# A 64-token tile's high and low parts side by side as one 128-column stationary, in a streaming encoder layer

## The chip, the cores and the metric

The kernel runs on one core of a Trainium2 chip. The metric is the device time of one execution in microseconds. Three runs of the kernel before took 2988.57, 2991.18 and 2994.07 us; their median, 2991.18 us, is the time that the prediction starts from. One further execution was recorded by the hardware profiler; its span, from the first to the last instruction, is 2988.4 us.

## What is computed

One layer of a streaming encoder, in float32, for 2048 prompt tokens and 64 sample tokens, with a model width of 1024:

```python
h = rms_norm(x, norm1_g) * (1 + sc1) + sh1
z = h @ w_in                                  # GLU pair, q, k, v, two gates
conv_out, conv_state = conv_module(u, conv_hist, ...)
attn_out = attend(q, k, v).reshape(B, T, ATTN_DIM) @ w_attn_out
merged = sigmoid(g_conv) * conv_out + sigmoid(g_attn) * attn_out
x = x + gt1 * (merged @ w_o)                  # output projection
h2 = rms_norm(x, norm2_g) * (1 + sc2) + sh2
gate, up = split(h2 @ w_ffn_in)
x = x + gt2 * ((silu(gate) * up) @ w_ffn_out) # second FFN product
```

Prompt and sample have vectors of their own for the modulation (`sc1` to `gt2`) and share all weights. The two lines with a comment on the right behind `x =` are those that the change touches, and of their rows only the 64 sample tokens.

## The kernel before

**Products in three passes.** Matmuls run in the format fp32r, whose operands hold fewer bits than float32. So each operand is kept as two tensors: `hi`, the value rounded by an ACT copy, and `lo`, what is left, which DVE (or POOL, for weights) makes by a subtraction (`split`, lines 706 to 709; `Weights.split`, lines 451 to 505, for weights). A product is then three matmuls into the same PSUM bank, hi by hi, hi by lo and lo by hi (`mm3`, lines 700 to 704); lo by lo is left out. Each of the three loads its stationary operand anew.

**Two parts.** The first part (to line 1657) computes the input projection, the convolution and the attention in four token blocks and stores gates and mixer outputs in HBM. The second part (from line 1660) goes over three blocks, `CBLOCKS`: tokens 0 to 576, 576 to 1344 and 1344 to 2112. Tokens 0 to 63 are the sample; they are a tile of their own, of 64 tokens, in the first block. All other tiles have 128. The first block has five tiles, the others six each.

**A block of the second part** (the loop at line 1802) has these steps:

- *Merge and output projection*, in two chunks of tiles. For each of eight groups of 128 channels, `merge` (lines 1677 to 1699) multiplies the mixer outputs `cin` by their weights, applies the gates, and splits the result into `m[0]` (hi) and `m[1]` (lo), 128 channels by the tokens of the chunk. `wo` (lines 1836 to 1846) takes a tile's columns of `m` as the stationary operand and 512 columns of `w_o` as the moving one; the PSUM banks are called `pw`. In the first chunk of the first block the tiles are 64, 128 and 128 tokens.
- *Residual* (lines 1710 to 1796), one generator for each tile: DVE multiplies the two banks by `gt1`, adds `x`; ACT squares and sums; DVE and POOL make the reciprocal root; ACT scales; PE transposes the tile to channels by tokens; ACT and DVE modulate and split it. For the sample tile the transposes are `pt<-ident,xn` of 64x64.
- *First FFN product* (`up`, lines 1926 to 1980), row by row: 22 rows of 128 hidden channels, `f`. Each row is made by a Strassen-like scheme for two by two blocks, with the tokens split into two halves of 288 (first block) or 384; the sample tokens are in half 0. The results are called `y` and `z` and lie in PSUM banks (`ps`). `hidden` (lines 1900 to 1903) splits a row's half into the tile `hid`, hi and lo, 128 channels by tokens.
- *Second FFN product*. In the first block (`add_down`, lines 2136 to 2168) two rows at a time: for each tile and each of two 512-column halves of `w_ffn_out`, 2 x 3 matmuls with `hid` as the stationary operand into a bank called `pd`, which ACT copies (first pair) or DVE adds (all later ones) into `acc` in SBUF. The last four rows are done together at the end of the block; there DVE adds `acc`, multiplies by `gt2`, adds `x1`, and the tile is written out. The other two blocks do most rows by `down_pair`, which the change does not touch.

**What sets the order.** PE's program order is written by the code as it runs. `Meter` estimates each operation's time as it is recorded, `Stream` keeps a clock for each engine, and the lanes' generators (weight loads, residual steps and others) are advanced when their due time has come on PE's clock. Whether the low part of a weight is made by POOL or by DVE is decided by the same clocks (line 483). A scheduler below then places instructions by readiness. So a change of a few matmuls also moves other instructions nearby. Loads and stores go by the queue of SP, in its own order.

Weights wait in HBM; they are loaded raw into staging buffers, split into `whi` and `wlo`, of which five pairs exist, and a pair comes free when PE has done its last matmul with it.

The functions that the diff touches:

Of the kernel before, what the change touches and what calls it, by code (L numbers as in the profile page):

```python
# [8 lines left out]
F32 = mybir.dt.float32  # L9
# [9 lines left out]
KT = 8  # L19
# [592 lines left out]
def streaming_layer(ctx: ExitStack, tc: tile.TileContext, I, O):  # L612
# [87 lines left out]
    def mm3(ps, lh, ll, rh, rl, first, last, **kw):  # L700
        pe.matmul(ps, lh, rh, start=first, stop=False, **kw)
        pe.matmul(ps, lh, rl, start=False, stop=False, **kw)
        pe.matmul(ps, ll, rh, start=False, stop=last, **kw)
        stream.spend()

    def split(hi, lo, src):
        act.activation(hi, src, AF.Copy)
        stream.after("dve", "act")
        dve.tensor_tensor(lo, src, hi.bitcast(F32), ALU.subtract)
# [966 lines left out]

    def merge(c0, c1, src, m, ahead, load):
        n = c1 - c0
        for ct in range(KT):
            g = ahead.pop(0)  # L1680
            if ct == 2 and load:
                load()
            wh, wl = W.get(("ca", ct))
            ps = [
                columns(
                    kts(wh, 4 * j, 4 * j + 4), kts(wl, 4 * j, 4 * j + 4), kts(src[0][j], 0, 4), kts(src[1][j], 0, 4), 0, n
                )[:, :n]
                for j in range(2)
            ]
            t = piece("t1", "t1")[:, :n]  # L1690
            stream.after("dve", "pe")
            dve.scalar_tensor_tensor(t, g[0][:, :n], 1.0, ps[0], ALU.add, ALU.mult)
            dve.scalar_tensor_tensor(ps[1], g[1][:, :n], 1.0, ps[1], ALU.add, ALU.mult)
            W.done()
            if ct + 2 < KT:
                ahead.append(gate_columns(c0, c1, ct + 2))
            dve.scalar_tensor_tensor(ps[1], ps[1], 2.0, t, ALU.mult, ALU.add)
            stream.after("act", "dve")
            split(m[0][:, ct, :n], m[1][:, ct, :n], ps[1])


    Y = ("y0", "z0", "y1", "z1")
# [7 lines left out]
    def residual(pp, t, n, gt1, a, half, hs, free, last, i):  # L1710


        which = int(t < SMP)
        x_t = [wk.tile([P, 512], F32, tag="ws", name="x_t", bufs=4) for _ in range(2)]
        for j in range(2):
            nc.sync.dma_start(x_t[j][:n], rows(x_p, x_s, t, n)[:, 512 * j : 512 * j + 512])
        yield
        x1 = token_row("x1")
        for j in range(2):
            f = slice(512 * j, 512 * j + 512)  # L1720
            stream.after("dve", "pe")
            dve.tensor_tensor(pp[j][:n], pp[j][:n], gt1[which][:n, f], ALU.mult)
        hs["rows"] -= 1
        yield
        for j in range(2):
            f = slice(512 * j, 512 * j + 512)
            dve.tensor_tensor(x1[:n, f], pp[j][:n], x_t[j][:n], ALU.add)
        free()
        yield stream.when("dve")
        xn = token_row("xn")  # L1730
        ssq = wk.tile([P, 1], F32, tag="ssq", bufs=2)
        act.activation(xn[:n], x1[:n], AF.Square, accum_out=ssq[:n])
        nc.sync.dma_start(x1_d[t : t + n], x1[:n])
        yield stream.when("act")
        r = rsqrt_mean(wk, ssq[:n], n, 1, D, 4)

        W.behind = lambda ins=gps.last.ins: tc.issue_after(ins)
        yield stream.when("pool")
        stream.after("act", "pool")
        act.activation(xn[:n], x1[:n], AF.Copy, scale=r)  # L1740
        yield stream.when("act")

        pts = pp if last else [bank_of(Y[i % 2 * 2 + j], "pt") for j in range(2)]
        pts = [pt.rearrange("p (k n) -> p k n", k=4) for pt in pts]
        for kk in range(KT):
# [12 lines left out]
        hs["columns"] -= 1  # L1758
        yield stream.when("dve", "act")
        for c, e, o in ((0, min(n, half - a), a), (max(0, half - a), n, max(0, a - half))):  # L1760
            if c >= e:
                continue
            b = [x[:, :, c:e] for x in cols_]
            at = lambda name: [hs[name][j][:, :, o : o + e - c] for j in range(2)]
            as_f32 = lambda name: [x.bitcast(F32) for x in at(name)]
            if a + c < half:
                for g in range(2):
                    split(*at("b%d1" % (g + 1)), b[g])
                    yield stream.when("dve")
# [12 lines left out]
            act.activation(at("b22")[0], b[1], AF.Copy)  # L1782
            for x in as_f32("b11"):
                dve.tensor_tensor(b[0], b[0], x, ALU.subtract)
            dve.tensor_tensor(at("t3")[1], t, as_f32("t3")[0], ALU.subtract)
            dve.tensor_tensor(t, b[1], b[0], ALU.subtract)
            yield stream.when("dve")
            split(*at("t2"), t)
            split(*at("t1"), b[0])
            yield stream.when("dve")  # L1790
            dve.tensor_tensor(b[0], as_f32("b21")[0], t, ALU.subtract)
            dve.tensor_tensor(b[0], b[0], as_f32("b21")[1], ALU.add)
            dve.tensor_tensor(at("b22")[1], b[1], as_f32("b22")[0], ALU.subtract)
            yield stream.when("dve")
            split(*at("t4"), b[0])
            yield stream.when("act")
# [5 lines left out]
    for s, (lo, hi) in enumerate(CBLOCKS):  # L1802
# [4 lines left out]
        for i, (c0, c1) in enumerate(chunks):  # L1807
# [28 lines left out]
            def wo(i, k):  # L1836
                (t, n), pp = grp[i], pss[i]
                if k not in ws:
                    ws[k] = W.get(("wo", k))
                wh, wl = ws[k]  # L1840
                c = slice(t - c0, t - c0 + n)
                for j in range(2):
                    f = slice(512 * j, 512 * j + 512)
                    mm3(pp[j][:n], m[0][:, k, c], m[1][:, k, c], wh[:, 0, f], wl[:, 0, f], k == 0, k == KT - 1)
                if i == len(grp) - 1:
                    W.done()

# [50 lines left out]
            return hid[i][:, f % 2]  # L1898

        def hidden(f, i, ps):  # L1900
            hi, lo = (hid_of(f)[:, j, i * half : (i + 1) * half] for j in range(2))
            stream.after("act", "dve")
            split(hi, lo, ps)

        class Operands:

# [229 lines left out]
        def add_down(fs, ws):  # L2136

            last = fs[-1] == NF - 1
            for i, (t, n) in enumerate(tiles):
# [6 lines left out]
                for e, j in [(e, j) for e in fs for j in range(2)] if last and not i else [(e, j) for j in range(2) for e in fs]:  # L2146
                    h = hid_of(e)
                    f = slice(512 * j, 512 * j + 512)
                    w = ws[e - fs[0]]
                    mm3(pss[j][:n], h[:, 0, c], h[:, 1, c], w[0][:, 0, f], w[1][:, 0, f], e == fs[0], e == fs[-1])  # L2150
                for j, ps in enumerate(pss):
                    f = slice(512 * j, 512 * j + 512)
                    dst = acc[i][:n, f]
                    stream.after("dve", "pe")
                    if fs[0] == 0:
                        act.activation(dst, ps[:n], AF.Copy)
                    elif not last:
                        dve.tensor_tensor(dst, dst, ps[:n], ALU.add)
                    else:
                        dve.tensor_tensor(ps[:n], ps[:n], dst, ALU.add)  # L2160
                        dve.tensor_tensor(ps[:n], ps[:n], gt[:n, f], ALU.mult)
                        dve.tensor_tensor(dst, ps[:n], x1[j], ALU.add)
                        stream.at(
# [91 lines left out]
```

## Time and profile before

| | us |
|---|---|
| Runs | 2988.57, 2991.18, 2994.07 |
| Median of the runs | 2991.18 |
| Span of the profiled execution | 2988.4 |
| PE busy in it | 2911.8 |
| DVE busy in it | 2025.1 |
| ACT busy in it | 1355.2 |
| POOL busy in it | 1140.8 |

The page gives no other time of the profiled execution than its span. Busy time of PE counts matmuls, whose modelled ends overlap: a matmul of 512 columns is listed with some 0.39 us although the next one starts 0.23 us later. PEld are the weight loads, which run beside the matmuls. All engine instructions are recorded by one helper, so all have line 102; they are told apart by the names of their tiles: `pw` is the output projection, `pd` the second FFN product, `ps` the products of merge and first FFN product, `cin` the mixer outputs, `whi` and `wlo` the split weights, `wst`, `wup`, `wfo` and `ws` the raw weights and their sums, `tg<-g_d` the loads of gates. An entry such as `128*64 128x512` is a matmul with 128 rows and 64 columns of the stationary operand and 512 moving columns. In brackets stands how long the engine sat idle before an instruction and what ended it.

The first block of the second part runs from about 1194 to 1725 us of the span.

### The profile page before, as it was taken

How to read it: one execution, taken by the hardware profiler on the slowest of the kernel's cores; microseconds unless marked ns; L12 is line 12 of the kernel's file. 1: busy time of each engine (PE TensorE's matmuls, PEld its weight loads, DVE VectorE, ACT ScalarE, POOL GpSimd, SP SyncE). 2: the span in 40 equal slices, each digit the busy share in tenths (PEclk: the TensorE clock that was granted, in tenths of full speed). 3: DMA queues.
4: the chain of work that ended last, by engine and by line, in shares of the span. 5: the costliest groups of instructions: out<-in, count | busy, mean ns of one | idle time of the engine just before them, and what ended most of it. 6: DMA issues, size and time to landing. Idle time of an engine off the chain costs nothing. (4 is left out here: it accounts for less than half of the span.)

```text
span 2988.4 us, 44911 instructions
## 1 busy us (share of the span) xinstructions
PE 2911.8 (97%) x16259; PEld 2594.0 (87%) x16259; DVE 2025.1 (68%) x3596; ACT 1355.2 (45%) x2437; POOL 1140.8 (38%) x734
## 2 busy tenths in 40 slices
PE   7999899999999999989999999999999999999999
PEld 4899777787888788878989899999999999999998
DVE  5897687668857885477777755666666657466666
ACT  3345643661465257464444335534444345344442
POOL 0201310111011102444666443255766741465667
PEclk9999999999999999999999999999999999999999
DMA  9989889978987888885444786323333975233333
GB/s 307 305 289 299 271 288 304 280 254 276 304 272 222 278 253 277 267 280 167 139 148 151 231 266 223 132 90 113 113 106 115 307 245 183 95 96 115 115 103 127
DMA packets 467725, 628.06 MB, mean 210 GB/s; under 512 B 36277, under 2 KB 314665, under 8 KB 467502
## 3 DMA queue, kind: packets, MB, share of 16 engines
q1 hardware_dynamic: 453456, 605.58, 62.7%
q10 hardware_dynamic: 14045, 19.60, 1.9%
q8 instruction: 128, 2.10, 0.3%
q14 instruction: 96, 0.78, 0.1%
HBM read 476.53 MB, written 148.54 MB: 209 GB/s over the span
## 5 line engine op out<-in xcount | busy, mean ns | idle before, releaser
L102 PE MATMUL ps<-t,whi 128*128 128x384 f32 (+1 forms) x2112 | 502.6, 322 | 10.3 <-ACT t L102 4.9
L102 POOL TENSOR_TENSOR wlo<-wst,whi 128x1024 fp32r<-128x1024 f32 (+1 forms) x157 | 357.8, 2289 | 288.6 <-ACT whi L102 256.3
L102 ACT ACTIVATE whi<-wst 128x1024 fp32r<-128x1024 f32 (+1 forms) x264 | 257.4, 977 | 335.6 <-PE ps L102 115.9
L102 PE MATMUL ps<-b,whi 128*128 128x384 f32 (+1 forms) x1584 | 381.4, 326 | 6.1 <-DVE early L102 3.3
L102 PEld LDWEIGHTS ps<-t,whi 128*128 128x128 f32 x2112 | 367.5, 188 | 17.8 <-ACT t L102 5.1
L102 DVE SCALAR_TENSOR_TENSOR y<-u,wd,y 128x512 f32<-128x512 f32 (+1 forms) x480 | 369.1, 773 | 6.3
L102 PE MATMUL ps<-hh,whi 128*128 128x512 f32 (+2 forms) x992 | 361.6, 365 | 0.0
L102 DVE TENSOR_TENSOR acc<-acc,pd 128x512 f32<-128x512 f32 (+1 forms) x464 | 311.6, 685 | 67.5 <-PE pd L102 64.8
L102 PE MATMUL ps<-hl,whi 128*128 128x512 f32 (+2 forms) x992 | 345.6, 348 | 0.0
L102 PE MATMUL ps<-hh,wlo 128*128 128x512 f32 (+2 forms) x992 | 345.1, 348 | 0.0
L102 PE MATMUL ps<-t,wlo 128*128 128x384 f32 (+1 forms) x1056 | 339.3, 321 | 1.0 <-POOL wlo L102 0.7
L102 PE MATMUL pd<-whi,hid 128*128 128x512 f32 (+1 forms) x1016 | 325.0, 391 | 0.0
L102 PEld LDWEIGHTS ps<-b,whi 128*128 128x128 f32 x1584 | 278.5, 189 | 12.0 <-DVE early L102 4.2
L102 POOL TENSOR_TENSOR r<-t,mhalf 128x1 f32<-128x1 f32 (+3 forms) x68 | 83.6, 1231 | 455.8 <-DVE t L102 450.6
L102 PE MATMUL ps<-b,wlo 128*128 128x384 f32 (+1 forms) x792 | 256.9, 325 | 0.0
L102 ACT ACTIVATE pr<-pr,sm 128x640 f32<-128x640 f32 (+3 forms) x272 | 200.2, 747 | 109.0 <-DVE sm L102 106.3
L102 PEld LDWEIGHTS pd<-whi,hid 128*128 128x128 f32 (+1 forms) x1016 | 185.9, 183 | 44.5 <-ACT hid L102 0.7
L102 PEld LDWEIGHTS ps<-hh,wlo 128*128 128x128 f32 x992 | 186.7, 188 | 21.8
L102 PEld LDWEIGHTS ps<-hh,whi 128*128 128x128 f32 x992 | 187.2, 189 | 18.6 <-issue 1.6
L102 PEld LDWEIGHTS ps<-hl,whi 128*128 128x128 f32 x992 | 187.5, 189 | 15.6 <-issue 1.4
L102 PEld LDWEIGHTS ps<-t,wlo 128*128 128x128 f32 x1056 | 198.2, 188 | 2.5 <-POOL wlo L102 1.3
L102 PE MATMUL pd<-wlo,hid 128*128 128x512 f32 (+1 forms) x508 | 198.4, 391 | 0.0
(225 smaller groups left out, 6174.2 us busy)
## 6 DMA issues: line engine op xcount, KB each, us to landing
whi<-w_din_h SPq DMA_DIRECT2D x72, 512.0 KB, 6.9
wlo<-w_din_l SPq DMA_DIRECT2D x72, 512.0 KB, 8.5
wst<-sum_d SPq DMA_DIRECT2D x132, 256.0 KB, 2.7
wfo<-in_w_ffn_out SPq DMA_DIRECT2D x64, 512.0 KB, 3.4
wmod<-in_w_ada SPq DMA_DIRECT2D x46, 512.0 KB, 6.2
sum_d<-ws SPq DMA_DIRECT2D x88, 256.0 KB, 3.2
wst<-in_w_ffn_in SPq DMA_DIRECT2D x84, 256.0 KB, 3.1
wst<-in_w_in SPq DMA_DIRECT2D x40, 512.0 KB, 8.5
```

What stands on the lines that cost most here:

```text
L102: self.last = f(*args, **kw)
```

## The change

In the first block, for the sample tile alone, hi and lo are put side by side: 64 columns of lo, then 64 columns of hi, as one stationary operand of 128 columns (`mm2`). Two matmuls, by hi and by lo of the weights, give hi by hi and hi by lo in partitions 64 to 127 of the bank, and lo by hi and lo by lo in partitions 0 to 63. At the end `fold` adds the two halves: ACT copies partitions 64 to 127 to SBUF, partitions 0 to 63, and DVE adds that to the bank. In `residual` the copy goes to the row `x1`, which is written later anyway; in the second FFN product the sum over rows is kept with all 128 partitions in `acc` and folded once, at the last rows.

To get the layout, the tiles `m[0]` and `hid` begin with the sample's lo, and all hi columns move 64 to the right. The low part of a chunk or half with sample tokens is now made by two DVE instructions: 64 columns into the front of the hi tile, and the rest, as before, into the lo tile.

```diff
+    def mm2(ps, both, rh, rl, first, last, **kw):
+
+        pe.matmul(ps, both, rh, start=first, stop=False, **kw)
+        pe.matmul(ps, both, rl, start=False, stop=last, **kw)
+        stream.spend()
+
+    def fold(ps, t):
+
+        stream.after("act", "pe")
+        act.activation(t, ps[SMP : 2 * SMP], AF.Copy)
+        stream.after("dve", "act")
+        dve.tensor_tensor(ps[:SMP], ps[:SMP], t, ALU.add)
...
     def merge(c0, c1, src, m, ahead, load):
         n = c1 - c0
+        cut = 0 if c0 else SMP
...
-            split(m[0][:, ct, :n], m[1][:, ct, :n], ps[1])
+            hi = m[0][:, ct, cut : cut + n]
+            act.activation(hi, ps[1], AF.Copy)
+            stream.after("dve", "act")
+            if cut:
+                dve.tensor_tensor(m[0][:, ct, :cut], ps[1][:, :cut], hi[:, :cut].bitcast(F32), ALU.subtract)
+            dve.tensor_tensor(m[1][:, ct, cut:n], ps[1][:, cut:], hi[:, cut:].bitcast(F32), ALU.subtract)
...
             f = slice(512 * j, 512 * j + 512)
+            if t < SMP:
+                fold(pp[j], x1[:n, f])
             stream.after("dve", "pe")
             dve.tensor_tensor(pp[j][:n], pp[j][:n], gt1[which][:n, f], ALU.mult)
...
-                    mm3(pp[j][:n], m[0][:, k, c], m[1][:, k, c], wh[:, 0, f], wl[:, 0, f], k == 0, k == KT - 1)
+                    if t < SMP:
+                        mm2(pp[j], m[0][:, k, : 2 * SMP], wh[:, 0, f], wl[:, 0, f], k == 0, k == KT - 1)
+                    else:
+                        mm3(pp[j][:n], a[:, c], m[1][:, k, c], wh[:, 0, f], wl[:, 0, f], k == 0, k == KT - 1)
...
         def hidden(f, i, ps):
...
+            if s:
+                split(h[:, 0, c], h[:, 1, c], ps)
+                return
+            hi = h[:, 0, SMP:][:, c]
+            act.activation(hi, ps, AF.Copy)
+            stream.after("dve", "act")
+            cut = 0 if i else SMP
+            if cut:
+                dve.tensor_tensor(h[:, 0, :cut], ps[:, :cut], hi[:, :cut].bitcast(F32), ALU.subtract)
+            dve.tensor_tensor(h[:, 1, c][:, cut:], ps[:, cut:], hi[:, cut:].bitcast(F32), ALU.subtract)
...
-                    mm3(pss[j][:n], h[:, 0, c], h[:, 1, c], w[0][:, 0, f], w[1][:, 0, f], e == fs[0], e == fs[-1])
+                    if t < SMP:
+                        mm2(pss[j], h[:, 0, : 2 * SMP], w[0][:, 0, f], w[1][:, 0, f], e == fs[0], e == fs[-1])
+                    else:
+                        a = h[:, 0, 0 if s else SMP :]
+                        mm3(pss[j][:n], a[:, c], h[:, 1, c], w[0][:, 0, f], w[1][:, 0, f], e == fs[0], e == fs[-1])
...
-                        act.activation(dst, ps[:n], AF.Copy)
+                        act.activation(dst, ps, AF.Copy)
                     elif not last:
-                        dve.tensor_tensor(dst, dst, ps[:n], ALU.add)
+                        dve.tensor_tensor(dst, dst, ps, ALU.add)
                     else:
-                        dve.tensor_tensor(ps[:n], ps[:n], dst, ALU.add)
+                        dve.tensor_tensor(ps, ps, dst, ALU.add)
+                        dst = dst[:n]
+                        if t < SMP:
+                            fold(ps, dst)
```

The tiles `m` and `hid` keep their sizes. Blocks 1 and 2, `down_pair` and the first FFN product's matmuls are as before.

More of the change, by code (lines that the diff above doesn't have):

```diff
@@ L1841, in wo @@
                 c = slice(t - c0, t - c0 + n)
+                a = m[0][:, k, 0 if c0 else SMP :]
                 for j in range(2):
                     f = slice(512 * j, 512 * j + 512)
-                    mm3(pp[j][:n], m[0][:, k, c], m[1][:, k, c], wh[:, 0, f], wl[:, 0, f], k == 0, k == KT - 1)
+                    if t < SMP:
+                        mm2(pp[j], m[0][:, k, : 2 * SMP], wh[:, 0, f], wl[:, 0, f], k == 0, k == KT - 1)
+                    else:
+                        mm3(pp[j][:n], a[:, c], m[1][:, k, c], wh[:, 0, f], wl[:, 0, f], k == 0, k == KT - 1)
                 if i == len(grp) - 1:
@@ L1900, in hidden @@
         def hidden(f, i, ps):
-            hi, lo = (hid_of(f)[:, j, i * half : (i + 1) * half] for j in range(2))
+            h = hid_of(f)
+            c = slice(i * half, (i + 1) * half)
             stream.after("act", "dve")
-            split(hi, lo, ps)
+            if s:
[8 more added lines that the diff above has]
+            dve.tensor_tensor(h[:, 1, c][:, cut:], ps[:, cut:], hi[:, cut:].bitcast(F32), ALU.subtract)
         class Operands:
@@ L2149, in add_down @@
                     w = ws[e - fs[0]]
-                    mm3(pss[j][:n], h[:, 0, c], h[:, 1, c], w[0][:, 0, f], w[1][:, 0, f], e == fs[0], e == fs[-1])
+                    if t < SMP:
[3 more added lines that the diff above has]
+                        mm3(pss[j][:n], a[:, c], h[:, 1, c], w[0][:, 0, f], w[1][:, 0, f], e == fs[0], e == fs[-1])
                 for j, ps in enumerate(pss):
                     f = slice(512 * j, 512 * j + 512)
-                    dst = acc[i][:n, f]
+                    dst = acc[i][:, f]
                     stream.after("dve", "pe")
                     if fs[0] == 0:
-                        act.activation(dst, ps[:n], AF.Copy)
+                        act.activation(dst, ps, AF.Copy)
                     elif not last:
-                        dve.tensor_tensor(dst, dst, ps[:n], ALU.add)
+                        dve.tensor_tensor(dst, dst, ps, ALU.add)
                     else:
-                        dve.tensor_tensor(ps[:n], ps[:n], dst, ALU.add)
+                        dve.tensor_tensor(ps, ps, dst, ALU.add)
+                        dst = dst[:n]
+                        if t < SMP:
+                            fold(ps, dst)
                         dve.tensor_tensor(ps[:n], ps[:n], gt[:n, f], ALU.mult)
```

## The prediction

> **What bounds the kernel now.** I read the page first, then busy time by stage, the chain of waits through the stage that is changed, and the timelines of PE and DVE there.
>
> ```profile
> span 2988.4 us, 44911 instructions
> PE 2911.8 (97%) x16259; PEld 2594.0 (87%) x16259; DVE 2025.1 (68%) x3596; ACT 1355.2 (45%) x2437; POOL 1140.8 (38%) x734
> PE 46%; DVE 1%; ACT 1%; issue 0%; DMA 0%; POOL 0%; SPq 0%; ACTq 0%; DVEq 0%; POOLq 0%
> ```
>
> TensorE is busy for 97% of the span and the chain that ended last is almost all PE. The page has a span of 2988.4 us and no other time for the profiled execution; the median of the runs is 2991.18, 2.8 us above it. I make the sum on the span and subtract it from the median.
>
> The change touches only the first block of the second part. Its stages, by busy time (sample projection, transition, early FFN, one steady FFN period, last product); the columns are us, busy time of PE, PEld, DVE, ACT and POOL with counts, PE clock, DMA share, GB/s:
>
> ```profile
> 1219.00:1250.00 31.00, 31.00 (x152) 24.05 (x151) 12.09 (x21) 8.71 (x11) 9.03 (x4) 1.00 0.96 277
> 1306.00:1357.00 51.00, 40.64 (x277) 38.78 (x276) 41.13 (x72) 29.47 (x61) 23.72 (x19) 0.93 0.78 269
> 1357.00:1414.00 57.00, 55.93 (x330) 48.81 (x329) 42.42 (x67) 24.80 (x47) 27.09 (x20) 1.00 0.51 161
> 1522.33:1558.54 36.21, 36.08 (x228) 32.85 (x229) 25.86 (x38) 14.69 (x31) 21.41 (x15) 1.00 0.43 134
> 1697.83:1725.13 27.30, 27.30 (x121) 21.32 (x120) 20.82 (x33) 3.04 (x5) 5.20 (x3) 1.00 1.07 354
> ```
>
> Where the two products run, PE has next to no idle time; only 1306 to 1357, which the change does not enter, has 10 us of it. So a matmul less there is time less, as long as no other engine's chain comes forward. The chain of waits shows which one is near:
>
> ```profile
> 1533.56 13.66 PE pd L102 x60
> 1547.22 6.20 PE ps L102 x47
> ...
> 1554.19 0.98 DVE wlo L102
> 1555.16 0.37 DVE hid L102
> 1555.53 1.33 DVE wlo L102
> ...
> 1558.54 11.20 PE ps L102 x83
> ```
>
> A steady period (two rows of the FFN) is 36.2 us: matmuls, the 60 of the second product (`pd`) among them, then a side chain of 5.1 us that starts when PE has let go of a weight buffer and runs through ACT and DVE back to PE. While it runs, PE does other matmuls, and it wins only just:
>
> ```profile
> 1557.98 0.30 PE L102 MATMUL ps<-t,wlo 128*128 128x288 f32 x1
> 1558.11 0.29 PE L102 MATMUL ps<-b,whi 128*128 128x288 f32 x1
> 1558.54 0.53 PE L102 MATMUL ps<-t,whi 128*128 128x288 f32 x2
> ```
>
> Starts are 0.13 apart, and then 0.43: PE loses 0.3 to 0.4 us there, once a period. All else of the period is PE's own.
>
> **The change part by part.** First, the matmuls that go:
>
> ```profile
> L102 PE MATMUL pd<-whi,hid 128*64 128x512 f32 x88 | 29.2, 394 | 0.0
> L102 PE MATMUL pd<-wlo,hid 128*64 128x512 f32 x44 | 17.2, 391 | 0.0
> L102 PE MATMUL pw<-whi,m 128*64 128x512 f32 x32 | 10.7, 391 | 0.0
> ```
>
> The sample tile has 88 + 44 = 132 matmuls in `pd` (22 rows x 2 halves x 3) and 32 + 16 = 48 in `pw` (8 x 2 x 3): 60 products of three. Each becomes two, so 60 matmuls go. The 390 ns are pipelined durations; the price is the distance between starts:
>
> ```profile
> 1533.63 0.39 PE L102 MATMUL pd<-wlo,hid 128*64 128x512 f32 x1
> 1534.32 0.39 PE L102 MATMUL pd<-wlo,hid 128*64 128x512 f32 x1
> ...
> 1536.39 0.39 PE L102 MATMUL pd<-wlo,hid 128*128 128x512 f32 x1
> 1536.39 0.42 PEld L102 LDWEIGHTS pd<-whi,hid 128*128 128x128 f32 x2
> 1537.08 0.39 PE L102 MATMUL pd<-wlo,hid 128*128 128x512 f32 x1
> ```
>
> One product of three with a 64-column stationary takes 0.69 us, with a 128-column one 0.69 as well (13.66 / 60 = 0.228 each over the whole `pd` stretch). A half-wide stationary is no cheaper; the 512 moving columns set the pace. The new form has the size of the 128-column rows: 2 x 0.228 = 0.456 instead of 0.69, 0.234 less. **60 x 0.234 = 14.0 us**: 3.7 in the projection, 10.3 in the FFN (0.94 a period). Weight loads start with the matmul before and end inside its 0.228, wide or narrow; two wide ones take 0.42, as quoted, against 2 x 0.228 of matmuls.
>
> What is added. **The low part is split in two** (64 columns into the stationary, the rest as before): 22 more DVE instructions at `hidden`, 8 at `merge`.
>
> ```profile
> L102 DVE TENSOR_TENSOR hid<-ps,hid 128x288 fp32r<-128x288 f32 x44 | 20.0, 454 | 15.5 <-ACT hid L102 15.4
> L102 DVE TENSOR_TENSOR acc<-acc,pd 128x512 f32<-128x512 f32 x448 | 301.9, 685 | 67.5 <-PE pd L102 64.8
> ```
>
> From the two, 1.03 ns a column and 157 ns fixed, so one instruction more is at most 0.157 us. But back to back, `hid` holds the chain for 0.37 (quoted above), not 0.454, so some 0.08 overlap with the neighbour; the added one delays by 0.07 to 0.16. In each of the seven steady periods one such split lies on the side chain. Since PE already loses time at its end, this shows in full: 7 x 0.08 (the `hid` row of the chain is the nearest) = **0.6 us** (0.5 to 1.1). The other split of the period and those of `merge` lie beside PE work: DVE is busy 25.9 of 36.2. If that cover failed, all 30 would cost 4.7 at most.
>
> **`fold`**: twice an ACT copy of 64x512 and a DVE add, in `residual` and in the last `add_down`.
>
> ```profile
> L102 ACT ACTIVATE other<-po 64x512 f32<-64x512 f32 x32 | 19.0, 593 | 55.0 <-PE po L102 54.7
> 1246.09 1.38 DVE L102 TENSOR_TENSOR pw<-pw,gt 64x512 f32<-64x512 f32 x2 [6.56 <-PE pw L102]
> 1250.69 1.15 ACT L102 ACTIVATE xn<-x,r 64x1024 f32<-64x1024 f32 x1 [0.84 <-POOL r L102]
> 1252.80 0.71 PE L102 MATMUL pt<-ident,xn 64*128 64x64 f32 x8
> ```
>
> The sample tile's way to its transposes gets 0.6 + 1.3 = 1.9 us longer (one copy, two adds). It ended at 1251.84, 0.96 before PE turned the tile. In the instruction order of the changed kernel the transposes stand 36 matmuls behind the tile's last product instead of 27: 8.2 us later instead of 6.2, so 2.0 cover the 1.9. DVE there holds the `ssq` step behind the next tile's first multiplication, which waits for PE until 5.5 us after; that leaves **0.5 us** (0 to 2). In the last product DVE needs 2 x 3.4 = 6.8 us for the sample tile (four steps of 0.7 and the copy, twice) where PE needs 5.5 for the next tile; the first half's bank is free after 3.4 and the second is asked for at 8.2: nothing. The ACT copies stand ahead of the weight split that waits for PE there.
>
> **What moves.** PE's last 6364 instructions stand in the same order; those of the other engines change only in this block and its seam. In the first FFN rows seven low-part splits go from POOL to DVE, two of 1024 columns and five of 512, where DVE is busy 42 of 57 us:
>
> ```profile
> 1551.52 0.69 DVE L102 TENSOR_TENSOR wlo<-ws,whi 128x512 fp32r<-128x512 f32 x1 [0.31 <-ACT whi L102]
> 1555.45 1.41 DVE L102 TENSOR_TENSOR wlo<-ws,whi 128x512 fp32r<-128x512 f32 x1
> 1561.44 1.68 DVE L102 TENSOR_TENSOR wlo<-wfo,whi 128x1024 fp32r<-128x1024 f32 x1 [0.49 <-ACT whi L102]
> ```
>
> By these, 7 to 10 us of DVE work, against 14 idle; I charge **0.5 us** (0 to 4). And at the seam PE comes 8 x 0.234 = 1.9 us sooner to the next merge, while the DMA engines are full (1.07 above):
>
> ```profile
> 1726.63 1.06 ACT L102 ACTIVATE whi<-wup 128x1024 fp32r<-128x1024 f32 x1 [2.39 <-DMA wup<-in_w_attn_out]
> 1742.04 0.55 DVE L102 SCALAR_TENSOR_TENSOR t<-tg,ps 128x384 f32<-128x384 f32 x1 [1.87 <-DMA tg<-g_d]
> ```
>
> ACT and DVE already wait for loads there, PE not yet. I charge **0.4 us** (0 to 1.9).
>
> Sum: -14.0 + 0.6 + 0.5 + 0.5 + 0.4 = -12.0, and 2991.2 - 12.0 = **2979.2 us**. With all costs at their low end -13.5; if the 0.3 to 0.4 of the side chain also went, -16. With all at the high end, -14.0 + 1.1 + 2 + 4 + 1.9 = -5.0, or 2986.2.
>
> **The rivals.** *Smaller gain*: the engines beside PE take half of it back: each added split costs 0.157 and the moved splits their high end. 30 x 0.157 + 4 = 8.7, and 2991.2 - 14.0 + 8.7 = 2985.9; halfway to the forecast lies 2982.5. For it speaks that the side chain already ends last; against it, that only one split a period lies on that chain.
>
> *No gain in the FFN*: the period of 36.2 is held by the supply of weights, and the 0.94 a period turn into waiting. Left are projection and last product, (16 + 8) x 0.234 = 5.6, less 1.4 for fold, moves and seam: 2987.0. Against it: the chain goes back through `pd` itself, and POOL is busy 21.4 of 36.2.
>
> *Slower*: DVE's weight splits collide with POOL. In the rows above the same 512-column split takes 0.69 or 1.41. Two of them lie on the side chain (0.98 and 1.33); a PE that arrives 0.94 earlier shifts them against POOL. If each met a full 1024-column split of POOL,
>
> ```profile
> 1524.17 2.41 POOL L102 TENSOR_TENSOR wlo<-wfo,whi 128x1024 fp32r<-128x1024 f32 x1
> ```
>
> they would take up to 0.69 + 2.41 = 3.1 each, 3.9 more a period, 27 in seven: 2991.2 - 12.0 + 27 = 3006. It decides from (12.0 + 6.0) / 7 = 2.6 us a period on. Against it: splits and the side chain start from the same PE releases, so most of the pattern moves along. The Trainium skill states such a rule (SBUF — State Buffer, "SBUF: two separate sides"): a DVE instruction with two SBUF inputs and a GpSimd one that reads SBUF exclude each other for a whole instruction. By that rule the blocked one waits out the other; the trace bears out that splits get longer, but POOL's get longer too, and no row here shows a DVE split of 512 columns at 3 us. Not touched by this is the added instruction, which reads PSUM: `hid` keeps its 0.45.
>
> That the change does not do what it says can be left aside: 60 matmuls less stand in the instruction order.
>
> **How the numbers follow.** Forecast (2975.5 to 2983) 0.72, smaller gain (2983 to 2986) 0.16, none in the FFN 0.08, slower 0.04. About 0.2%, 6 us, is what a measurement can tell from no change: the line is 2985.2. Faster: 0.72 and most of the second, 0.87; same 0.09; slower 0.04. The range 2975.5 to 2985.5 leaves out the last two and a bit of the second.
>
> **What would show it.** `pd` at 56 matmuls and 12.7 us a period, and the period at 35.2 to 35.4; `pw` and `pd` starts still 0.228 apart; the wait of PE for ACT `u` at the period's end grown by about 0.1, not by 0.9; the blocks behind this one as long as before. A period still at 36.2, DVE splits of 2 us on the chain, or PE waiting for loads behind the last product would prove me wrong.

## The result and the profile after

The changed kernel took 2980.65 us (median of five runs, 2978.88 to 2983.51) against 2991.18 us (2988.57 to 2994.07) for the kernel before on the same chip: a ratio of 0.996, with a 95% interval of 0.9949 to 0.9971, or 8.7 to 15.3 us less. The forecast of 2979.2 us lies 1.5 us below the median. The profiled execution has a span of 2977.7 us, 10.7 less than that of before.

The page of the changed kernel, its first lines and its chain by engine:

```profile
span 2977.7 us, 44838 instructions
PE 2900.2 (97%) x16199; PEld 2593.1 (87%) x16199; DVE 2025.9 (68%) x3637; ACT 1356.8 (46%) x2441; POOL 1127.7 (38%) x727
PE 82%; DVE 7%; DMA 4%; ACT 2%; issue 2%; POOL 2%; SPq 0%; ACTq 0%; POOLq 0%; DVEq 0%
```

PE has 60 matmuls less and 11.6 us less of busy time; DVE has the 30 small splits and the four adds of `fold`, and seven weight splits that POOL no longer makes. The chain reads 82% PE where it read 46% before. The two can't be compared: the shares of before add up to 48% and those of after to 99%, so the chain of before was followed back through only half of the span, and that it is "almost all PE" holds for this half. PE was busy for 97% in both.

The groups of PE by line and form (count, busy us, mean ns) show the new shape. Before there were four groups with `128*64`; now all is `128*128`, with 44 + 44 + 16 + 16 = 120 matmuls more where 180 narrow ones are gone:

```profile
L102 PE MATMUL pd<-whi,hid 128*128 128x512 f32 x972 | 314.8, 390 | 0.0
L102 PE MATMUL pd<-wlo,hid 128*128 128x512 f32 x508 | 198.6, 391 | 0.0
L102 PE MATMUL pw<-whi,m 128*128 128x512 f32 x528 | 166.6, 391 | 0.0
L102 PE MATMUL pw<-wlo,m 128*128 128x512 f32 x272 | 106.0, 390 | 0.0
```

Busy time by stage of the changed kernel, with the columns that the prediction named (a stretch of the early FFN rows, a steady period, the start of the next block):

```profile
1362.00:1419.00 57.00, 55.38 (x343) 50.49 (x342) 39.63 (x67) 23.32 (x43) 22.64 (x16) 1.00 0.47 154
1483.53:1518.75 35.22, 35.10 (x225) 32.67 (x225) 24.48 (x40) 14.72 (x31) 23.50 (x15) 1.00 0.46 147
...
1715.15:1749.08 33.93, 33.93 (x194) 33.93 (x193) 19.82 (x32) 13.69 (x17) 20.62 (x9) 1.00 1.01 326
```

The steady period is 35.22 us instead of 36.21. Behind the last product PE goes on into the next block without a gap, 33.93 of 33.93, at a DMA share of 1.01. The early FFN stretch has 1.6 us of idle PE; the same stretch of before had 1.1.

The chain of waits through the end of a steady period, as it was shown of before:

```profile
1515.37 0.43 DVE hid L102 x2
1515.81 1.27 DVE wlo L102
1517.08 0.38 DVE ps L102
...
1517.98 0.41 ACT hid L102
1518.39 0.31 ACT u L102
...
1518.75 11.21 PE ps L102 x83
```

The two `hid` instructions hold the chain for 0.43 where the one held it for 0.37. But the weight split behind them takes 1.27 there instead of 1.33, and what PE sees is unchanged. Its timeline at this place:

```profile
1518.33 0.29 PE L102 MATMUL ps<-b,whi 128*128 128x288 f32 x1
1518.75 0.53 PE L102 MATMUL ps<-t,whi 128*128 128x288 f32 x2
```

The starts are 0.42 apart; before it was 0.43.

**Where the time went.** From the starts of PE's matmuls, the span divides into what lies ahead of the block's first `merge` matmul, the block, and the rest. The block divides into projection (to the first FFN matmul), transition (to the first `pd`) and FFN (to the next block's first `merge` matmul). In us, for all profiled executions of this study:

| kernel | first part | projection | transition | FFN | block | rest | span |
|---|---|---|---|---|---|---|---|
| before | 1194.4 | 111.6 | 51.6 | 367.4 | 530.6 | 1263.4 | 2988.4 |
| before, again (e0) | 1198.7 | 111.1 | 51.6 | 368.1 | 530.8 | 1263.4 | 2992.9 |
| changed | 1199.2 | 107.7 | 51.6 | 356.5 | 515.8 | 1262.7 | 2977.7 |
| changed, again (e4) | 1201.4 | 107.1 | 50.8 | 356.4 | 514.4 | 1263.5 | 2979.2 |
| projection alone (e1) | 1198.1 | 107.2 | 50.8 | 368.3 | 526.2 | 1264.6 | 2988.9 |
| FFN alone (e2) | 1196.5 | 111.5 | 51.1 | 358.0 | 520.6 | 1265.3 | 2982.3 |
| all but the matmuls saved (e3) | 1195.7 | 112.5 | 51.3 | 368.5 | 532.3 | 1262.9 | 2990.9 |
| low part in 7 pieces (e5) | 1193.9 | 107.5 | 51.0 | 354.8 | 513.2 | 1263.4 | 2970.5 |
| low part in 14 pieces (e6) | 1197.5 | 107.2 | 44.7 | 360.4 | 512.2 | 1263.7 | 2973.4 |
| k and v too (e7) | 1212.7 | 107.4 | 51.9 | 357.0 | 516.2 | 1264.6 | 2993.5 |
| changed, `u` first (e8) | 1198.1 | 107.6 | 51.2 | 354.6 | 513.4 | 1263.9 | 2975.3 |
| before, `u` first (e9) | 1200.4 | 111.2 | 50.4 | 364.1 | 525.6 | 1264.1 | 2990.1 |
| changed, six temporaries (e10) | 1197.4 | 108.2 | 51.7 | 356.5 | 516.4 | 1264.6 | 2978.4 |

The block is 14.8 us shorter. The first part, whose code is the same in all of these but e7 and e10, ends anywhere from 1193.9 to 1201.4, and in the profiled pair it happened to be 4.8 longer after the change. That explains 14.8 in the block and 10.7 in the span, and it is why the verdicts below on a few us come from the block's stages, not from the span.

### The profile page after: what moved, and what is told of

Read it like the earlier page. It is cut to its first block, busy times and chain, and to the rows that moved or that the text cites. A ratio compares the mean times of both kernels' runs of the same rounds, so it can differ in the third digit from the quotient of the medians.

```text
span 2977.7 us, 44838 instructions
## 1 busy us (share of the span) xinstructions
PE 2900.2 (97%) x16199; PEld 2593.1 (87%) x16199; DVE 2025.9 (68%) x3637; ACT 1356.8 (46%) x2441; POOL 1127.7 (38%) x727
## 4 chain that ended last, share of the span: by engine, by line
PE 82%; DVE 7%; DMA 4%; ACT 2%; issue 2%; POOL 2%; SPq 0%; ACTq 0%; POOLq 0%; DVEq 0%
PE ps L102 53%; PE pd L102 16%; PE pw L102 6%; DVE y L102 2%; PE sc L102 2%; PE po L102 2%; PE ptp L102 2%; DVE wlo L102 1%; PE pt L102 1%; DMA kk<-k_d 1%; ACT whi L102 1%; PE pa L102 1%; POOL r L102 1%; DVE pw L102 1%; DMA wst<-in_w_in 0%
## 5 line engine op out<-in xcount | busy, mean ns | idle before, releaser
L102 POOL TENSOR_TENSOR wlo<-wst,whi 128x1024 fp32r<-128x1024 f32 (+1 forms) x156 | 356.4, 2294 | 279.0 <-ACT whi L102 262.6
L102 DVE TENSOR_TENSOR acc<-acc,pd 128x512 f32<-128x512 f32 x464 | 311.7, 685 | 62.7 <-PE pd L102 60.2
L102 PE MATMUL pd<-whi,hid 128*128 128x512 f32 x972 | 314.8, 390 | 0.0
L102 PEld LDWEIGHTS pd<-whi,hid 128*128 128x128 f32 x972 | 182.5, 188 | 37.7 <-ACT hid L102 0.7
L102 PE MATMUL pd<-wlo,hid 128*128 128x512 f32 x508 | 198.6, 391 | 0.0
```

What stands on the lines that cost most here:

```text
L102: self.last = f(*args, **kw)
```

## Experiments

**Theory:** the time comes from 60 matmuls less at 0.234 us each, and all that is added is hidden or nearly so. **Rivals:** the engines beside PE take a part of it back; or the gain comes from the order that the change happened to make elsewhere.

**e0, e4: the two kernels again.** No edit.

> The kernel before once more, for the first part of the span, whose code is the same in both kernels: the merge began at 1194.4 us before and at 1199.2 us after the change. If the start of a program varies from one execution to the next, this one lies some us away from 1194.4, and the runs with the changed code scatter as well. If the changed program itself is slower in its first part, this one is at 1194.4 within 0.5 and all with the changed code are near 1199.

> The changed kernel once more, timed on one chip with the kernel before. In two profiles of before the block lasts 530.6 and 530.8 us while the first part ends anywhere between 1194 and 1199. Theory: block 515.8 within 0.3, and the runs 12 to 16 us under before, since the two parts that vary by execution (the start, and one wait for gates near 2361 us) average out. Rival (the median gain of 10.5 is the true one and the 14.8 of the profile is chance): block 518 or more, runs 10 under before.

The kernel before agrees with itself to 0.3 us in the block and to 0.7 or better in each of its stages, and differs by 4.3 in the first part. The changed one again took 2978.62 us against 2991.61, ratio 0.9949 (0.9935 to 0.9963), and its block 514.4, 1.4 shorter than the first time where 0.3 was expected. So the change is worth 10.5 in one comparison of medians and 13.0 in the other; the block is 14.8 to 16.4 shorter, by which two profiles are compared.

**e1, e2: each half alone.** The edits take one half of the diff back, for e1 that of the FFN (its main lines):

```diff
...
-                    if t < SMP:
-                        mm2(pss[j], h[:, 0, : 2 * SMP], w[0][:, 0, f], w[1][:, 0, f], e == fs[0], e == fs[-1])
-                    else:
-                        a = h[:, 0, 0 if s else SMP :]
-                        mm3(pss[j][:n], a[:, c], h[:, 1, c], w[0][:, 0, f], w[1][:, 0, f], e == fs[0], e == fs[-1])
+                    mm3(pss[j][:n], h[:, 0, c], h[:, 1, c], w[0][:, 0, f], w[1][:, 0, f], e == fs[0], e == fs[-1])
...
```

> The change in the output projection alone; the second FFN product stays at three passes. Theory (a matmul less is 0.23 us less, the rest is hidden): 16 x 0.234 = 3.7 us off, all of it between the first merge matmul and the first FFN matmul, 111.6 us before and 107.9 here; the second FFN product from its first matmul to the next merge stays at 367.5; total 2987.4. Rival (the gain comes from other instructions that the planner moved, not from the count of matmuls): the two stretches do not divide as 3.7 to 0.

> The change in the second FFN product alone; the output projection stays at three passes. Theory: 44 x 0.234 = 10.3 us off, between the first matmul of the second FFN product and the next merge, 367.5 before and 357.2 here; the stretch from the first merge matmul to the first FFN matmul stays at 111.6; total 2980.9. Rival (the reordering did it): not this division. Together with the projection alone the two gains should add up to that of the whole change if the pieces do not help each other.

e1: 2990.84 against 2992.0 us, ratio 0.9995 (0.9986 to 1.0004); its block is 4.3 shorter than that of before, 4.4 of it in the projection, and the FFN is 0.9 longer, of which 0.7 is what the two profiles of before differ by. e2: 2984.07, ratio 0.9972 (0.9962 to 0.9982); its block is 10.0 shorter, 9.4 of it in the FFN. The parts add up to 14.3 of the whole's 14.8. In the total, e1 can't be told from no change, since 4 us is what the first part varies by; its projection stage can.

**e3: everything but the matmuls saved.** Layout, split and `fold` stay; `mm2` issues a third matmul with the weights' low part again, so the sample's result gets its small terms twice.

```diff
         pe.matmul(ps, both, rh, start=first, stop=False, **kw)
+        pe.matmul(ps, both, rl, start=False, stop=False, **kw)
         pe.matmul(ps, both, rl, start=False, stop=last, **kw)
```

> All of the change (side by side layout, split low parts, folds), but with a third matmul in each product of the sample tile, by the low part of the weights again; so the sample's result gets these small terms twice. It has before's 16 + 44 = 60 matmuls back and shows all that the change costs without what it saves. Theory (all costs hidden): 2991 within 1 us of before, both stretches within 0.6 us of before. Rival 1 (the costs are those forecast, 2.0 in all): 2993. Rival 2 (the order of instructions is what gained): part of the 10 us stays, below 2988.

2992.57 us, ratio 1.0001 (0.9991 to 1.0011); block 532.3, 1.8 above before and 1.6 above its repeat. With the matmuls back, all of the gain is gone, so neither the layout nor what comes with it gains by itself. What is added costs these 1.6 to 1.8 in that kernel, near the 2.0 of the forecast. The order of instructions is not held fixed by this: e3 has an order of its own, with three weight splits moved from POOL to DVE where the changed kernel has seven.

**e5, e6: a longer split on the side chain.** The change left PE's wait at the end of the period as it was, although one DVE instruction more lies on the chain there. To see how much fits, the second part of `hid`'s low part (224 columns) is made in 7 pieces of 32 columns, or in 14 of 16:

```diff
-            dve.tensor_tensor(h[:, 1, c][:, cut:], ps[:, cut:], hi[:, cut:].bitcast(F32), ALU.subtract)
...
+            for a in range(cut, half, 32):
+                e = slice(a, a + 32)
+                nc.vector.tensor_tensor(h[:, 1, c][:, e], ps[:, e], hi[:, e].bitcast(F32), ALU.subtract)
```

> The changed kernel with the 224-column low part of half 0 made by seven DVE instructions of 32 columns in place of one, same result. In the side chain the low parts then take some 0.35 us longer and the next weight split starts later. Theory (that split cannot end before the POOL instruction that holds it back, so what is added ahead of it is absorbed): steady periods stay at 35.2 to 35.3. Rival (an added instruction adds its length to the chain, as I forecast): 35.6 a period, 2.5 us in seven.

> The same with fourteen instructions of 16 columns, some 0.8 us longer than with one, which brings the weight split to the end of POOL's instruction at hand. Theory: the split then starts behind POOL's next instruction and waits for that one as well, so the period jumps, by 1 us or more (36.2 and above), not by what was added less the slack. Rival (added length adds): 36.0, and half of that step already with seven.

One execution of each took 2972.41 and 2975.2 us, inside the range of the changed kernel's five runs on the same chip (2972.2 to 2981.0). Their steady periods are 34.9 us against its 35.2, so neither got longer and none of the expected periods came out. (In e6 four `pd` matmuls run 7.2 us ahead of the others, so its line between transition and FFN lies elsewhere, and only its block compares.) For the seven pieces the absorption at the weight split is plain. From the timelines of three kernels (DVE and POOL rows of one stretch each), first before:

```profile
1554.57 1.75 POOL L102 TENSOR_TENSOR wlo<-wst,whi 128x512 fp32r<-128x512 f32 x1
1555.09 0.45 DVE L102 TENSOR_TENSOR hid<-ps,hid 128x288 fp32r<-128x288 f32 x1
...
1555.45 1.41 DVE L102 TENSOR_TENSOR wlo<-ws,whi 128x512 fp32r<-128x512 f32 x1
```

then the changed kernel:

```profile
1514.79 1.74 POOL L102 TENSOR_TENSOR wlo<-wst,whi 128x512 fp32r<-128x512 f32 x1
...
1515.30 0.51 DVE L102 TENSOR_TENSOR hid<-ps,hid 128x64 fp32r<-128x64 f32 x2
...
1515.73 1.35 DVE L102 TENSOR_TENSOR wlo<-ws,whi 128x512 fp32r<-128x512 f32 x1
```

and the one with seven pieces:

```profile
1542.94 1.75 POOL L102 TENSOR_TENSOR wlo<-wst,whi 128x512 fp32r<-128x512 f32 x1
...
1543.46 0.21 DVE L102 TENSOR_TENSOR hid<-ps,hid 128x64 fp32r<-128x64 f32 x1
...
1543.60 0.76 DVE L1944 TENSOR_TENSOR hid<-ps,hid 128x32 fp32r<-128x32 f32 x7
1544.28 0.96 DVE L102 TENSOR_TENSOR wlo<-ws,whi 128x512 fp32r<-128x512 f32 x1
```

From the start of `hid` to that of the weight split it is 0.36, 0.43 and 0.82: some 0.065 for each instruction more. The weight split starts later and takes 1.41, 1.35 and 0.96. It ends at 1556.86, 1517.08 and 1545.24, that is 0.54, 0.55 and 0.55 after the end of POOL's split (1556.32, 1516.53, 1544.69). So it isn't DVE that sets this moment but POOL, and the added instructions fill a time in which DVE was held up anyway. The Trainium skill (SBUF — State Buffer, "SBUF: two separate sides") says that a DVE instruction with two inputs in SBUF and a GpSimd one that reads SBUF hold their shared port for a whole instruction each, the other waiting; the trace agrees, and also with the exception: `hid`, which reads PSUM, goes through while POOL's split runs. Whether the absorption ends where it should, when `hid` lasts past POOL's end, 1.2 us behind its own start, was not learned: in both kernels the scheduler had also put the ACT instruction `u` ahead of `hid`, and the wait was gone altogether. My expectation of a jump for the 14 pieces failed for that reason.

**e8, e9: the exchange alone.** In the seven-piece kernel ACT's copy `u` stands ahead of `hid` of the row before; in the changed kernel it stands behind. e8 makes this exchange in the changed kernel, in six periods, and e9 in the kernel before, with nothing else:

```diff
-            if late:
+            if late and s:
                 rest(*late.pop())
             u2 = piece("t1", "u2")[:, :half]
             keep = (lambda dst, ps: plus(dst, ps, s1)) if f < EARLY else copy
             keep(u2, y)
+            if late:
+                rest(*late.pop())
```

> The changed kernel with one pair of ACT instructions exchanged in six of the seven steady periods: the copy u, for which PE waits, ahead of hid of the other half of the row before (in the changed kernel hid 1517.98, then u 1518.29, and PE's next start 0.42 after the last). If PE's wait at the end of the side chain is only this place in ACT's queue, PE has no gap of 0.42 there any more, the period falls from 35.23 to 34.9 as in the run with seven pieces, the FFN stage from 356.4 to about 354.5, and the time by 6 x 0.3 = 1.8 us, to about 2977 to 2979. If the wait is set by the DVE instruction ahead of hid (the sum in ps at 1517.08 and its end), u in front of hid waits just as long for its own turn and period and time stay as they are. If hid, now 0.3 later, holds up the products of the next second FFN pair, the period grows instead: 35.5 and more, 2 us slower.

> The kernel before with the same exchange in ACT's order and nothing else. If the wait of 0.43 at the end of its periods is the same one, its period falls from 36.20 to 35.9 and its time by about 2 us, to a ratio of 0.9993; the change then had nothing to do with this wait, neither made nor cured it. If the wait in the kernel before has another cause (the sum hid on DVE, one instruction instead of two), nothing moves.

e8: 2974.89 us against 2995.27, ratio 0.9936 (0.9923 to 0.9948); its FFN stage is 354.6, 1.8 less than the changed kernel's, as expected. e9: 2988.58, ratio 0.998 (0.997 to 0.999); FFN 364.1, 3.3 less than before, where 2 were expected. ACT's timeline of the changed kernel,

```profile
1516.87 1.06 ACT L102 ACTIVATE whi<-wfo 128x1024 fp32r<-128x1024 f32 x1 [1.08 <-issue]
1517.98 0.41 ACT L102 ACTIVATE hid<-ps 128x288 fp32r<-128x288 f32 x1
1518.29 0.41 ACT L102 ACTIVATE u<-ps 128x288 f32<-128x288 f32 x1
```

and of e8, one place exchanged:

```profile
1514.70 1.06 ACT L102 ACTIVATE whi<-wfo 128x1024 fp32r<-128x1024 f32 x1 [1.06 <-issue]
1515.67 0.39 ACT L102 ACTIVATE u<-ps 128x288 f32<-128x288 f32 x1
1515.96 0.40 ACT L102 ACTIVATE hid<-ps 128x288 fp32r<-128x288 f32 x1
```

`u` comes 0.97 after `whi` instead of 1.42. `u` reads a bank that only PE has written; it needs nothing of the side chain. It waited for DVE's last multiplication because `hid`, one place ahead in ACT's queue, did. The Trainium skill (PSUM — Partial Sum Buffer, "Engine vs sequencer instructions") calls ScalarE's queue a strict FIFO; the trace agrees, by the 1.42 against 0.97. In e8 the chain of waits has no engine but PE:

```profile
1499.83 5.44 PE pd L102 x24
1505.27 22.20 PE ps L102 x168
1527.47 12.92 PE pd L102 x56
...
```

The extra 1.3 of e9 has two parts, of which some 0.4 are lost again at the starts of three `pd` stretches. One, 0.7, lies in the last rows, where two waits for `u`, of 1.16 and 0.86 between starts, have become one of 1.35 for `v`. The other, 0.9, is a second wait with the same root. In one period of the kernel before, DVE's weight split starts 0.2 after POOL's and takes 1.62, where in the other periods it starts 0.05 to 0.08 ahead of POOL's and takes 0.69; all of the side chain is then 0.9 late. DVE, POOL and later PE rows of its timeline:

```profile
1514.16 1.28 POOL L102 TENSOR_TENSOR wlo<-wst,whi 128x512 fp32r<-128x512 f32 x1
...
1514.37 1.62 DVE L102 TENSOR_TENSOR wlo<-ws,whi 128x512 fp32r<-128x512 f32 x1 [0.59 <-ACT whi L102]
...
1521.01 0.29 PE L102 MATMUL ps<-b,whi 128*128 128x288 f32 x1
1522.33 0.53 PE L102 MATMUL ps<-t,whi 128*128 128x288 f32 x2 [1.03 <-ACT u L102]
```

PE loses 1.3 between two starts there, 0.9 more than in the other periods. It has lost 0.3 already at 1517.40, and the whole period is 37.43 where its neighbours are 36.18. In e9 the same collision is still to be seen,

```profile
1518.01 1.28 POOL L102 TENSOR_TENSOR wlo<-wup,whi 128x512 fp32r<-128x512 f32 x1
...
1518.21 1.62 DVE L102 TENSOR_TENSOR wlo<-ws,whi 128x512 fp32r<-128x512 f32 x1 [0.59 <-ACT whi L102]
...
1521.13 0.40 ACT L102 ACTIVATE s<-ps 128x288 f32<-128x288 f32 x1
...
1521.24 0.30 PE L102 MATMUL ps<-b,wlo 128*128 128x288 f32 x1
1521.58 0.53 PE L102 MATMUL ps<-t,whi 128*128 128x288 f32 x2
```

but the wait of 0.9 is gone: `u` no longer hangs on the side chain. The 0.3 remains (starts 0.34 apart above, 0.13 in the other periods): PE starts 0.05 after the end of ACT's copy `s`, which is late in that period as it was before. In the changed kernel DVE's split goes first and takes 0.69 in every steady period, and both waits have gone (e1, e2 and e3 still have them). That is 1.2 that the change gained by the order it fell into, not by its matmuls.

**e7, e10: the same trick in the first part.** The k and v products of the sample tile in two passes, 16 matmuls less. The wider tile needs room, so one of seven temporaries goes; e10 is the changed kernel with six temporaries and nothing else.

```diff
-            mm3(ps[:n], hh[:, k, c], hl[:, k, c], wh[:, k % 2], wl[:, k % 2], k == 0, k == KT - 1)
+            if t < SMP:
+                mm2(ps, hb[:, k, : 2 * SMP], wh[:, k % 2], wl[:, k % 2], k == 0, k == KT - 1)
+            else:
+                mm3(ps[:n], hh[:, k, c], hl[:, k, c], wh[:, k % 2], wl[:, k % 2], k == 0, k == KT - 1)
...
+            if t < SMP:
+                fold(ps, temp("low")[:n])
```

> The changed kernel with the same side by side stationary also for the sample tile in the first part's k and v products (2 x 8 products of three passes become two, eight extra 64-column DVE instructions, two folds), and one of seven temporary tiles less, since the memory is needed. Theory: PE is busy there too, so 16 x 0.234 = 3.7 us less than the changed kernel, 2977; the missing temporary and the longer way of the sample's k and v may take back up to 2. Rival (the first part is held by DMA, not by PE): no gain.

> The changed kernel with six instead of seven temporaries, and nothing else: the control for the run with the same trick in the k and v products, whose first part was 11 to 19 us longer. If the lost temporary was the cause, the first part ends here near 1212 as well and the time is about 2994. If the edit of the k and v products was, the first part ends at 1194 to 1201 as in the changed kernel, and the time is about 2980.

e7: 2995.56 us where 2977 were expected, ratio 1.0016 (1.0006 to 1.0025), slower than the kernel before; its block is as short as the changed kernel's, its first part 11 to 19 us longer. e10: 2978.21, ratio 0.9946 (0.9934 to 0.9959), its first part 1197.4. So the missing temporary by itself costs nothing, and the edit of k and v does, alone or together with it. Busy time of e7, from 500 to 600 us,

```profile
500.00:600.00 100.00, 93.81 (x467) 74.59 (x468) 75.31 (x137) 49.03 (x85) 12.07 (x11) 0.94 0.84 263
```

and of e10 over the same stretch,

```profile
500.00:600.00 100.00, 96.69 (x490) 79.85 (x489) 75.30 (x142) 55.99 (x99) 11.59 (x11) 1.00 0.88 278
```

show 23 matmuls less in 100 us and a granted clock of 0.94 instead of 1.00. PE's waits for `s` of POOL ahead of `pm` from 240 to 620 us are 10.9 us in e7 and 3.9 in e10, but those for `x_t` of DVE, 7.5 us in e10, are gone in e7. The edit moved much of the first part's order with it. Which of the new order, the wait for POOL or the lower clock is cause and which is effect stays open.

## Why the prediction was right, step by step

By the starts of PE's matmuls, the profile of before against that of after. The third column is the number of matmuls less times the forecast's 0.234; here the transition ends, and the early rows begin, with PE's last wait in the transition.

| stretch | matmuls less | by count | measured | left over |
|---|---|---|---|---|
| projection | 16 | -3.74 | -3.91 | -0.17 |
| transition | 0 | 0 | -0.08 | -0.08 |
| early FFN rows | 12 | -2.81 | -1.12 | +1.69 |
| six steady periods | 24 | -5.62 | -7.02 | -1.40 |
| last rows and last product | 8 | -1.87 | -2.67 | -0.80 |
| block | 60 | -14.04 | -14.80 | -0.76 |

- **The 60 matmuls at 0.234** held, and e1 to e3 show that they are the gain. The cleanest row is e2: it keeps the collision that the whole change lost, and its six steady periods are 5.56 shorter than those of before, against 5.62 by count; five of them, from `pd` to `pd`, are shorter by 0.95 to 0.97 each. A stationary operand of 64 columns took as long as one of 128, as the prediction read from the starts.
- **The split on the side chain, charged with 0.6**, cost nothing. The 0.06 were there (0.37 to 0.43), but the weight split behind it ends by POOL's clock; the chain as quoted before had shown its 1.33 against 0.69 elsewhere, and I didn't ask what ended it. That PE's wait would grow by 0.1 was wrong, it stayed at 0.42.
- **`fold` in the residual, charged with 0.5**: nothing that can be seen; the transition is 51.6 in both. Copies, additions and the tile's transposes in the changed kernel's timeline:

```profile
1247.41 1.08 ACT L102 ACTIVATE x<-pw 64x512 f32<-64x512 f32 x2 [2.06 <-PE pw L102]
1248.04 1.29 DVE L102 TENSOR_TENSOR pw<-pw,x 64x512 f32<-64x512 f32 x2 [5.06 <-ACT x L102]
1254.04 1.15 ACT L102 ACTIVATE xn<-x,r 64x1024 f32<-64x1024 f32 x1 [1.15 <-POOL r L102]
```

  The tile is ready at 1255.2 and PE turns it from 1255.9 on: the nine matmuls more ahead of the transposes did cover it.
- **The moved weight splits, charged with 0.5 (0 to 4)**, are the term that was too small, as far as the runs tell: the early rows gave back 1.7 of their 2.8 (2.1 in the repeat e4; the two profiles of before differ by 0.6 there). DVE, now with three weight splits in a row, comes late to the sum `v` (changed kernel's timeline),

```profile
1371.99 3.66 DVE L102 TENSOR_TENSOR wlo<-ws,whi 128x512 fp32r<-128x512 f32 x3 [8.54 <-ACT whi L102]
1375.58 0.44 DVE L102 TENSOR_TENSOR v<-ps,v 128x288 f32<-128x288 f32 x1
```

  and PE's waits from 1340 to 1465 us name it (us, times, longest; a wait of 1.6 for `u` is in both), in the kernel before

```profile
PE ps L102 <- DVE v L102: 0.6, 1, 0.6
PE ps L102 <- DVE hid L102: 0.5, 1, 0.5
PE ps L102 <- DVE wlo L102: 0.3, 1, 0.3
```

  and in the changed one:

```profile
PE ps L102 <- DVE v L102: 1.6, 2, 1.4
...
PE ps L102 <- ACT s L102: 0.8, 1, 0.8
```

  These waits grew by 1.0 in all; the rest of the 1.7 lies in gaps that the view does not name. No run moves the splits alone. In e1, whose FFN matmuls are those of before but which has three weight splits moved as well, the early rows are 1.2 longer; in e9, with three moved too, they are not.

- **The seam, charged with 0.4**: no wait appeared; PE is busy for 33.93 of 33.93 us behind it although the DMA share is 1.01.
- **What the sum lacked** is the other sign: waits that the kernel before had and the changed one lost, 1.4 in the steady periods, 1.2 of it the collision above, and 0.8 in the last rows, where PE waited 1.1 us for `u` and now waits 0.3. The prediction had read one period, not all seven, and so did not see that one of them was 1.2 longer than its neighbours.

So the mechanism was right, and the closeness of the total is in part luck. Costs of 2.0 were forecast, and the balance measured in the block is -0.8, made of +1.7 and -2.5: one cost was too small, the others did not appear, and a gain that nobody had forecast outweighed them. The block alone says 14.8 less, the medians 10.5 and 13.0, the forecast 12.0. The intervals of both comparisons (8.7 to 15.3 and 11.1 to 19.4 less) hold the 14.8, and the first part's spread of some 7 us is wide enough for the difference; that it is the reason was not shown run by run. Of the rivals, none came true in the whole: PE's time for the sample's products went down by the count, so the supply of weights does not hold the period (e8's is 34.9 to 35.2, with PE alone on its chain). The collision of DVE and POOL, the rival on the other side, is real but sits in the kernel before; its price was 1.2 once, not 3.9 in each period.

Of the versions with more than one run, e8, the change with `u` first, has the lowest ratio to the kernel before, 0.9936; the blocks of e5 and e6 (513.2 and 512.2 in one execution of each) are as short as its 513.4. Against the changed kernel it was not timed directly; on its chip e10, the changed kernel with one temporary less, had 0.9946, and the intervals overlap. That it gains on the changed kernel rests on its FFN stage, 1.8 less than in both profiles of that one.

## What to carry to other kernels

Price a matmul by the distance between starts, and look for stationary operands that are half filled: here 64 and 128 columns cost the same 0.23 us, and filling the second half with the low part made one pass of three superfluous. Where a chain of waits names a producer, ask whether the consumer needs what that producer waited for, or whether it only stands behind it in an in-order queue: one exchange in ACT's order was worth 1.8 and 3.3 us, and in the kernel before it took 0.9 off the 1.2 that a collision elsewhere cost. Compare stage by stage, and all periods of a loop rather than one, when other stages vary by more than the change is worth.

## What the runs showed of the hardware

- A DVE split of 512 columns takes 0.69 us alone. Behind a POOL instruction that has already begun it ends 0.54 to 0.55 after that one's end, in each of the five places listed above, whatever its own start (0.96 to 1.62 listed). Where DVE begins first, by 0.08, DVE's takes 0.69 and POOL's 1.77 instead of 1.28 (changed kernel's timeline):

```profile
1511.73 0.69 DVE L102 TENSOR_TENSOR wlo<-ws,whi 128x512 fp32r<-128x512 f32 x1 [0.31 <-ACT whi L102]
1511.81 1.77 POOL L102 TENSOR_TENSOR wlo<-wst,whi 128x512 fp32r<-128x512 f32 x1
```

- A DVE instruction more, back to back with its like, costs some 0.065 us, not the 0.157 that the difference of two sizes gave: the listed times of neighbours overlap (in the rows of seven pieces one starts at 1543.46 with 0.21, the next at 1543.60).
